# Mixers without zero-padded operands, heads in plane order, and small products issued in unbroken batches

## The chip, the cores and the metric

The kernel runs on one core of a Trainium2 chip. The metric is the device time of one execution in microseconds (us). Executions were repeated, and the median counts. Engines are named as in the profile: PE is TensorE, DVE VectorE, ACT ScalarE, POOL GpSimd, SP the engine that issues DMAs.

## What is computed

One layer of a streaming encoder, for 1024 new tokens of one stream and 32 tokens of a second, running stream: x plus a normed token mixer, then plus a normed causal ConvFFN. The mixer has three groups of heads side by side on one in-projection, and one out-projection behind them. Cut to what the change touches:

```python
# GLA (6 heads, 32 keys, 64 values) and HGRN2 (5 heads, 64 x 64): per chunk of 64 tokens
b = cumsum(log_a)                               # decay per key channel
scores = einsum('bihd,bjhd,bijhd->bijh', q, k, exp(b_i - b_j))   # for j <= i
o = scores @ v + (q * exp(b)) @ S
S = exp(b_last) * S + (k * exp(b_last - b)).T @ v
# mLSTM (5 heads, 64 x 64): per chunk, with a running maximum m
s = (q @ k.T) * w
num, den = s @ v + w0 * (q @ C), sum(s) + w0 * (q @ n)
h = num / max(|den|, exp(-m))
C, n = dc * C + (wk * k).T @ v, dc * n + sum(wk * k)
# every head: RMS norm, times a gate; then cat @ w_out
```

## The kernel before

**Stages.** The in-projection runs in three groups of tokens (0 to 383, 384 to 767, 768 to 1023 with the 32 sample tokens). Its large products are split into three fp32r products each (`mm3`, L100 to L102). In each group come first the blocks of features (`pf`: queries, keys, decays, written to DRAM as `qkb_d` and `mqk_d`), then the blocks by token (`pv`: values and gates, written to `v_d` and `g_d`). Then follow the out-projection (`zp`), the up-projection of the FFN as a Strassen product (`pu...`) and the down-projection (`pd`).

**Mixers.** A mixer is a generator that handles a unit of 128 tokens (two chunks of 64), unit 8 the 32 sample tokens. The order of units is 0, 1, 2, then 3, 4, 5, then 8, 6, 7. `merge` runs the mixers of one group's units beside the in-projection of the next group, and the last group's beside the out-projection: with each step of the main generator `pump` advances the mixers by a share of `NMIX` steps per unit (L1392). On this the scheduler of the program sets the final order per engine. A small product is recorded through `first` (L690 to L692, hence most are at L692), which raises its priority by AHEAD, 100.

**A unit.** It loads `qkb` (q, k and b of GLA and HGRN2, 768 KB, L703; one buffer), `mqk`, `v` and others. From b come `kh` (L758 to L761), transposed into `kt2`, and `qz` (L753). The scores within a chunk are formed by levels c = 32, 16, 8, 4, 2, 1: at each level b is taken relative to the middle of each block of 2c tokens (L802), then exponentials on ACT, then the two operands `Ld` (L807) and `Qz` (L813, L817) on DVE, 16 products into the bank pair `sc`, and a copy under a mask into `P` (`put`, L782). Only the second half of each block is a query, so a level's output has 32 columns per chunk and head. The diagonal, each token with itself, is a product `z` (L838), summed over keys into `sd` and copied into `P` too. Then come the updates of the state (`up` in the bank `mi`, S at L857 and L858), `P` times `v` into `og` (GLA) and `oh` (HGRN2), `qz` times the state into the same, and `finish` (ACT square, L888 sum, POOL power at L218 and L219, L890 product, L892 gate). Then the mLSTM: `sm` (scores), `w`, `kw2`, `um` (update of the memory), `om`, `oi`, `hn`, `finish`. The banks tagged "o" (`og`, `oh`, `sm`, `om`, `oi`) are two in all, `mi` is one bank of two halves.

**Padding.** A product whose head has 32 or 64 keys and uses part of the 128 rows has its operand padded with zeros to 128 rows: `qz` (11 heads), `mqz` (5), `kt2` and `kw2` (each chunk's tokens, zeros for the other chunk). So these products run on 128 rows by 64 or 32 columns; the levels run on 64 by 64.

## Time and profile before

| | |
|---|---|
| median of 3 runs | 1438.58 us (1437.68 to 1443.81) |
| span of the profiled execution, first to last instruction | 1434.5 us |
| mean granted TensorE clock in it | 0.984 |
| PE, DVE, ACT, POOL busy | 1370.8, 1008.9, 713.2, 274.1 us |
| mixers' small products in the trace | 187 to 635 us for the last level, first to last unit |

Of the profiled execution the profile gives the span alone; the three runs are other executions. How to read the lines below: a line of the timeline gives the start in us, the length, engine, line, operation, output and inputs, and the count of records put together. A line of a group gives, behind the count, busy time in all and the mean of one in ns, then the engine's idle time ahead of it and what ended it. In a product's line "64*64" is the part of the array that it uses, rows by columns, and an fp32 product shows as two records. Records of one engine overlap at their ends, so that the difference of two starts tells what one costs.

### The profile page before, as it was taken

The numbers are of one execution on the slowest core, as the hardware profiler recorded it, in microseconds if no ns is written. First come the engines' busy times: TensorE is split into PE (matmuls) and PEld (weight loads), VectorE is DVE, ScalarE is ACT, GpSimd is POOL, SyncE is SP. The second block draws the span as 40 slices with busy tenths as digits, with TensorE's granted clock in tenths as the row PEclk, the third lists the DMA queues.
The fourth block names the chain that finished last, engine by engine and source line by source line (L and its number), as shares of the span: only waits on it lengthen the run. The fifth ranks groups of instructions, "written<-read, shape, count | busy, mean of one in ns | idle before, by whom it ended". The sixth has DMA issues, their size and how long they took to land.

```text
span 1434.5 us, 30019 instructions
## 1 busy us (share of the span) xinstructions
PE 1370.8 (96%) x11804; PEld 1254.9 (87%) x11804; DVE 1008.9 (70%) x1826; ACT 713.2 (50%) x1403; POOL 274.1 (19%) x456
## 2 busy tenths in 40 slices
PE   7989999999998998999799999999999999999997
PEld 6989889898887986767699999999999999988785
DVE  5796478757596668676698888788878865654644
ACT  5545556445475545333665555455555545543432
POOL 6531121113021235212111111111111110000101
PEclk9999999999999999999899999999999999999999
DMA  9599778667789754344312221222122266665742
GB/s 344 190 317 351 263 251 300 221 228 241 236 279 329 250 181 148 109 147 111 122 49 98 79 90 61 90 75 82 68 90 75 75 211 227 222 214 170 247 168 103
DMA packets 132437, 255.11 MB, mean 178 GB/s; under 512 B 28647, under 2 KB 79367, under 8 KB 132295
## 3 DMA queue, kind: packets, MB, share of 16 engines
q1 hardware_dynamic: 132295, 253.19, 51.9%
q8 instruction: 92, 1.51, 0.4%
q14 instruction: 50, 0.41, 0.1%
HBM read 192.26 MB, written 60.89 MB: 176 GB/s over the span
## 4 chain that ended last, share of the span: by engine, by line
PE 73%; DVE 12%; ACT 5%; DMA 5%; issue 2%; POOL 1%; SPq 1%; DVEq 0%; ACTq 0%
PE pd L101 5%; PE pd L100 5%; PE pd L102 5%; PE pux L100 4%; PE pux L102 4%; PE pux L101 4%; PE pv L102 4%; PE pv L100 4%; PE pv L101 4%; PE puw L100 3%; PE puw L101 3%; PE puw L102 3%; DMA qkb<-qkb_d 2%; PE zp L100 2%; PE zp L101 2%
## 5 line engine op out<-in xcount | busy, mean ns | idle before, releaser
L1226 DVE SCALAR_TENSOR_TENSOR y<-uu,fconv_sb,y 128x1060 f32<-128x1060 f32 x88 | 116.2, 1321 | 27.4 <-ACT y L1224 26.6
L100 PE MATMUL pd<-wd,hh 128*128 128x512 f32 x264 | 104.5, 396 | 0.3 <-ACT hh L106 0.3
L101 PE MATMUL pd<-wd,hh 128*128 128x512 f32 x264 | 104.7, 397 | 0.0
L102 PE MATMUL pd<-wd,hl 128*128 128x512 f32 x264 | 90.5, 394 | 0.0
L1220 POOL COPY uu<-uu 128x2 f32<-128x2 f32 x44 | 30.5, 693 | 211.5 <-DVE uu L1188 211.4
L1183 ACT COPY c<-pux 128x274 f32<-128x274 f32 (+1 forms) x132 | 49.1, 375 | 41.4 <-PE pux L102 40.3
L1224 ACT ACTIVATE y<-uu,fconv_sb 128x1060 f32<-128x1060 f32 x44 | 56.1, 1275 | 18.6 <-POOL uu L1221 18.1
L100 PE MATMUL zp<-woh,ch 128*128 128x512 f32 (+1 forms) x144 | 58.3, 411 | 4.1 <-DVE cl L1020 3.1
L100 PEld LDWEIGHTS pd<-wd,hh 128*128 128x128 f32 x264 | 49.6, 188 | 13.1 <-ACT hh L106 0.9
L102 PEld LDWEIGHTS pd<-wd,hl 128*128 128x128 f32 x264 | 49.6, 188 | 11.9
L101 PEld LDWEIGHTS pd<-wd,hh 128*128 128x128 f32 x264 | 49.6, 188 | 11.5
L100 PE MATMUL pv<-wt_0h,xh 128*128 128x256 f32 (+2 forms) x195 | 57.1, 293 | 2.3 <-ACT xh L316 2.3
L101 PE MATMUL zp<-wol,ch 128*128 128x512 f32 (+1 forms) x144 | 58.6, 407 | 0.0
L102 PE MATMUL zp<-woh,cl 128*128 128x512 f32 (+1 forms) x144 | 58.0, 406 | 0.2 <-DVE cl L1020 0.2
L102 PE MATMUL pv<-wt_1h,xl 128*128 128x256 f32 (+2 forms) x195 | 56.9, 292 | 0.5 <-DVE xl L317 0.5
L102 PE MATMUL pv<-wt_0h,xl 128*128 128x256 f32 (+2 forms) x195 | 56.5, 290 | 0.6 <-DVE xl L317 0.6
L100 PE MATMUL pv<-wt_1h,xh 128*128 128x256 f32 (+2 forms) x195 | 56.7, 291 | 0.0
L101 PE MATMUL pv<-wt_1l,xh 128*128 128x256 f32 (+2 forms) x195 | 56.5, 290 | 0.0
L101 PE MATMUL pv<-wt_0l,xh 128*128 128x256 f32 (+2 forms) x195 | 56.2, 288 | 0.1
L101 PE MATMUL pd<-hl,wd 128*128 128x288 f32 x176 | 50.3, 297 | 0.6 <-DVE hl L109 0.6
L218 POOL TENSOR_SCALAR hrs<-hss 128x5 f32<-128x5 f32 (+3 forms) x27 | 13.9, 514 | 192.1 <-DVE hss L888 191.4
L102 PE MATMUL pd<-hh,wd 128*128 128x288 f32 x176 | 50.1, 296 | 0.0
(1668 smaller groups left out, 5162.7 us busy)
## 6 DMA issues: line engine op xcount, KB each, us to landing
h_d<-y SPq DMA_DIRECT2D x22, 530.0 KB, 2.9
wt_0r<-in_w_tok SPq DMA_DIRECT2D x21, 512.0 KB, 8.2
wt_1r<-in_w_tok SPq DMA_DIRECT2D x21, 512.0 KB, 5.6
wt_0l<-lt_d SPq DMA_DIRECT2D x14, 512.0 KB, 5.2
wt_1l<-lt_d SPq DMA_DIRECT2D x14, 512.0 KB, 4.6
qkb<-qkb_d SPq DMA_DIRECT2D x8, 768.0 KB, 6.3
hr<-h_d SPq DMA_DIRECT2D x44, 128.0 KB, 3.7
hr<-h_d SPq DMA_DIRECT2D x22, 192.0 KB, 3.3
```

The costliest lines, as they stand in the source:

```text
L100: pe.matmul(ps, lh[0], rh[0], start=first, stop=False, **kw)
L101: pe.matmul(ps, lh[0], rh[1], start=False, stop=False, **kw)
L102: return pe.matmul(ps, lh[1], rh[0], start=False, stop=last, **kw)
L218: pool.tensor_scalar(out, ss, 1.0 / width, EPS, op0=ALU.mult, op1=ALU.add)
L1183: act.copy(t, ps)
L1220: pool.tensor_copy(u[:, GAP_P:GAP_P + 2], u[:, GAP_S - 2:GAP_S])
L1224: act.activation(y, u, AF.Identity, scale=fconv[:, j, 2:3], bias=fconv[:, j, 3:4])
L1226: dve.scalar_tensor_tensor(y, uu[i][:, s:s + NCOL], fconv[:, j, s:s + 1], y, op0=ALU.mult, op1=ALU.add)
```

## The change

1. **Padding.** `qz`, `kt2`, `mqz`, `kw2` are gone. `qb` (L755, L757), `kt` and `kw` hold the operands once, and each product takes a slice of 64 rows (`up`: 64 rows by 32 columns, so that 22 products per unit become 32). Products of the two halves of the rows go to different banks (`up` one bank of `sc` per chunk, `sm`, `um`, `oi` two banks each, `og` for planes 0 to 5 and `oh` for 6 to 10). `P` times `v` and `om` keep their form.
2. **Plane order.** The 11 heads stand in the order of the planes of `P`; the columns of the weights are permuted on the host.
3. **Pairs.** `Ld` and `Qz` have four buffers. Two levels write side by side into one `sc` (32 columns each); their copies into `P` come behind both.
4. **Batches.** `batch` issues a pair's products and a group of others without a break: updates with `sm`; levels 32 and 16 with `um`; 8 and 4 with `oi` and `om`; 2 and 1 with `qb` times the state; and `P` times `v` alone, last. The diagonal comes behind the pair 2 and 1, `hn` ahead of it.
5. **Order.** AHEAD is 3000 instead of 100, NMIX 14 instead of 17. `mqk` comes in two loads instead of four.

```diff
-    Ld = [mx.tile([128, 4, 128], F32, name=f"Ld{i}") for i in range(2)]
-    Qz = [mx.tile([128, 6, 64], F32, name=f"Qz{i}") for i in range(2)]
-    qz = mx.tile([128, 11, 128], F32, name="qz")
-    kt2 = mx.tile([128, 2, 512], F32, name="kt2")
-    mqz = mx.tile([128, 5, 128], F32, name="mqz")
-    kw2 = mx.tile([128, 2, 5, 64], F32, name="kw2")
+    Ld = [mx.tile([128, 4, 128], F32, name=f"Ld{i}") for i in range(4)]
+    Qz = [mx.tile([128, 6, 64], F32, name=f"Qz{i}") for i in range(4)]
+    qb = mx.tile([128, 6, 128], F32, name="qb")
+    kt = mx.tile([128, 512], F32, name="kt")
+    kw = mx.tile([128, 5, 64], F32, name="kw")
...
-    AHEAD = 100
+    AHEAD = 3000
...
+        def batch(first_one, *rest):
+
+            gate = last = None
+            with tc.high_priority(offset=AHEAD):
+                gate = last = first_one()
+                with tc.issue_after(gate.ins):
+                    for part in rest:
+                        for one in part:
+                            last = one()
+            return last
...
-            spread(dve, qz, lambda r, fs, psl: dve.tensor_tensor(qz[r, psl, :n], q4[r, fs, :], eb4[r, fs, :],
-                                                                 op=ALU.mult), n)
+            dve.tensor_tensor(qb[:, 2:4, :n], eb4[:, 1:3, :], q4[:, 1:3, :], op=ALU.mult)
+            for i, f in enumerate((0, 3)):
+                dve.tensor_tensor(qb[:, 4 * i:4 * i + 2, :n], eb4[:, f:f + 1, :].broadcast_to([128, 2, n]),
+                                  qe[:, i, :, :n], op=ALU.mult)
...
+        ups = [mm(up[ch][r:r + 32, f, :], kt[o:o + m, 128 * f + r:128 * f + r + 32], v[o:o + m, 64 * p:64 * p + 64])
+               for p, (f, r0, dk) in reversed(list(enumerate(PLANES)))
+               for r in range(r0, r0 + dk, 32) for ch, (o, m) in enumerate(chunks)]
...
+        last = batch(ups[0], ups[1:], inner)
...
+        pairs = [levels[i:i + 2] for i in range(0, len(levels), 2)]
...
+        batch(lists[1][0], lists[1][1:], lists[0], inner)
+        for lv, c in enumerate(pairs[0]):
+            copy_scores(c, sc, lv)
...
+        last = batch(inter[0], inter[1:], *lists[::-1])
+        for lv, c in enumerate(pairs[2]):
+            copy_scores(c, sc, lv)
+        z = mx.tile([128, 512], F32, tag="x", name=f"x{u}_0", bufs=NX)
+        dve.tensor_tensor(z[:, :4 * n], q4.rearrange("p f n -> p (f n)"), k4.rearrange("p f n -> p (f n)"), op=ALU.mult)
+        sd = small(11)
+        with tc.issue_after(last.ins):
+            for f in range(4):
+                first(pe.matmul, sd[:n], z[:, f * n:f * n + n], of_head[:, f, :], start=f == 0, stop=f == 3)
+        put(0, sd[:n].unsqueeze(2).broadcast_to([n, 11, cl]))
...
+        intra = [mm(ots[p][0][o:o + m, ots[p][1], :], P[o:o + m, p, :m], v[o:o + m, 64 * p:64 * p + 64],
+                    start=False, stop=p in (5, 10)) for p in range(11) for (o, m) in chunks]
+        batch(intra[0], intra[1:])
...
-    NMIX, NIN = 17, 12 + 2 + 24
+    NMIX, NIN = 14, 12 + 2 + 24
```

How this moves instructions is seen at two places. On DVE between units 1 and 2, before: the copies of levels 2 and 1 (`sc1_2`, `sc1_1`) and of the diagonal (`mi`, 128x704) into `P`, the state S, and then `kh` of unit 2, which waits for the load of `qkb2`.

```order
L782 COPY_PREDICATED P_160<-masks_sb_108,sc1_2_3076 128x176x2 [waits PE_49]
L782 COPY_PREDICATED P_160<-masks_sb_108,mi_157 128x704 [waits DVE_49]
L389 SCALAR_TENSOR_TENSOR mo_1_2919<-th_1_2917,y_1_2912 128x384 [waits DMAHW0_49,Activation_49]
L782 COPY_PREDICATED P_160<-masks_sb_108,sc1_1_3135 128x352 [waits DVE_49,PE_49]
L858 TENSOR_TENSOR S1_0_3206<-S1_0_3206,mi_157 128x256 [waits PE_49]
L857 TENSOR_TENSOR S1_1_3220<-S1_0_3206,dec1_2780 128x256 [waits DVE_49]
L758 TENSOR_TENSOR kh2_3612<-qkb2_3556 128x512 [waits DMAHW6_49]
L802 TENSOR_TENSOR x2_32_3629<-qkb2_3556 128x512
```

The same place after the change (`sc1_2` is now the third bank pair, with levels 2 and 1; the copies are at L816, `kh` at L762 and L765, `qb` at L755 and L757):

```order
L937 TENSOR_TENSOR cat1_3334<-hn1_3337,hrs1_3336 128x320 [waits DVE_49,Pool_49]
L816 COPY_PREDICATED P_163<-masks_sb_108,sc1_2_3341 128x176x2 [waits PE_49]
L816 COPY_PREDICATED P_163<-masks_sb_108,sc1_2_3341 128x352 [waits DVE_49]
L762 TENSOR_TENSOR kh2_3699<-qkb2_3631 128x512 [waits DMAHW6_49]
L816 COPY_PREDICATED P_163<-masks_sb_108,mi_160 128x704 [waits DVE_49,PE_49]
L830 TENSOR_TENSOR x2_32_3830<-qkb2_3631 128x512
L749 COPY dec2_3694<-eb2_3692 128x8 [waits Activation_49]
L755 TENSOR_TENSOR qb_156<-eb2_3692,qkb2_3631 128x256
L757 TENSOR_TENSOR qb_156<-eb2_3692,qe2_3687 128x256 x2
L765 TENSOR_TENSOR kh2_3699<-kh2_3699,qkb2_3631 128x512 [waits Activation_49]
```

The subtraction for `kh2` now stands ahead of the copy of unit 1's diagonal. The same holds between units 2 and 3 and between 3 and 4; between 4 and 5, 8 and 6, and 6 and 7 the diagonal's copy stands ahead.

On PE, unit 2's last level and first update of the state before (`mi` from `v2` and `kt2`), inside big products (`pv`):

```order
L692 MATMUL sc2_1_3980<-Qz1_151,qkb2_3556 64x2x32 [waits DVE_49]
L692 MATMUL sc2_1_3980<-Qz1_151,qkb2_3556 64x2x32 x3
L692 MATMUL sc2_1_3980<-Qz1_151,qkb2_3556 64x32 x8
L692 MATMUL sc2_1_3980<-Qz1_151,qkb2_3556 64x2x32
L692 MATMUL sc2_1_3980<-Qz1_151,qkb2_3556 64x32
L692 MATMUL sc2_1_3980<-Qz1_151,qkb2_3556 64x2x32
L692 MATMUL sc2_1_3980<-Qz1_151,qkb2_3556 64x32
L692 MATMUL mi_157<-v2_3563,kt2_153 32x64 [waits DVE_49]
L692 MATMUL mi_157<-v2_3563,kt2_153 32x64 x5
L692 MATMUL mi_157<-v2_3563,kt2_153 64x64 x5
L102 MATMUL pv5_5_3839<-wt1_5_0h_3715,xl1_1716 128x256
```

After, the updates of both chunks come as one run of 32, with `sm` of both halves of the rows (`sm20`, `sm21`) behind them, ahead of all levels:

```order
L85 MATMUL pv4_3_3350<-wt1_3_1l_3303,xh1_1716 128x256
L780 MATMUL up2_3742<-v2_3636,kt_157 32x64 [waits DMAHW2_49,Activation_49]
L780 MATMUL up2_3742<-v2_3636,kt_157 32x64 x31
L780 MATMUL sm20_3740<-mqk2_3633 64x64 [waits DMAHW1_49,DVE_49]
L780 MATMUL sm20_3740<-mqk2_3633 64x64
L780 MATMUL sm21_3741<-mqk2_3633 64x64 [waits DVE_49,PE_49]
```

`sm20` waits for VectorE too: it takes a bank "o" that the unit before it frees with its `finish`. Over the whole program the places at which the big products are left for products of another tile fall from 120 to 73, and the changes of tile shape from 384 to 175. The mixers move closer together: counted in big products, unit 1 begins at 1329, 2 at 1460, 3 at 1607 and ends at 1689 (before 1200 to 1434, 1488 to 1752, 1776 to 2024), unit 0 lies between 596 and 692 (before 888 to 1131), and units 5, 8, 6 and 7 between 2396 and 2688 (before 2256 to 2823).

More of the change, by code (lines that the diff above doesn't have):

```diff
@@ L74 @@
 SCW = 88
-HCOL = [64 * (0, 2, 1, 3, 4)[i] for i in range(5)]
 VG0 = [range(0, 3), range(3, 6), range(6, 8)]
@@ L777, in put @@
+        yield
         def put(c, src):
[L778 removed]
+            mk_ = masks[:n, lev_index[c]:lev_index[c] + 1, :cl]
             dst = P[:n, :, :cl]
             if c:
[L781 to L788 removed]
@@ L790, in mixer, with level @@
-        li = 0
-        for c in levels:
+                mk_, dst, src = second(mk_, c), second(dst, c), src.rearrange("p h (b c) -> p h b c", c=c)
+            dve.copy_predicated(dst, mk_.broadcast_to([n, 11, *mk_.shape[2:]]), src)
+        def level(li, c, sc, lv):
             x = mx.tile([128, 512], F32, tag="x", name=f"x{u}_{c}", bufs=NX)
@@ L874, in mixer, with scores @@
-        if u in (7, 8):
-            sp.dma_start(a["p_gh" if u == 7 else "q_gh"], state["S", u == 8])
+                put(c, s[:n])
+        def scores(k):
+            sc = psm.tile([128, 1024], F32, tag="sc", name=f"sc{u}_{k}", bufs=1)
+            return sc[:, :11 * SCW].rearrange("p (h s) -> p h s", s=SCW)
+        pairs = [levels[i:i + 2] for i in range(0, len(levels), 2)]
+        ums = [psm.tile([128, 3, 65], F32, tag="o", name=f"um{u}{e}", bufs=2) for e in range(2)]
+        sc = scores(0)
@@ new lines, in mixer @@
+        lists = []
+        for lv, c in enumerate(pairs[0]):
+            lists.append(level(lv, c, sc, lv))
+            if not lv:
+                yield
+        inner = [mm(ums[ch][64 * (h % 2):64 * (h % 2) + 64, h // 2, :], kw[o:o + m, h, :], vmt[o:o + m, h, :])
+                 for h in range(5) for ch, (o, m) in enumerate(chunks)]
+        batch(lists[1][0], lists[1][1:], lists[0], inner)
+        for lv, c in enumerate(pairs[0]):
+            copy_scores(c, sc, lv)
+        yield
+        w = mx.tile([128, 320], F32, tag="w", name=f"w{u}", bufs=1)
@@ new lines, in mixer @@
+        if u in (7, 8):
+            sp.dma_start(a["p_c" if u == 7 else "q_c"], state["C", u == 8])
+        yield
+        sc = scores(1)
+        lists = []
+        for lv, c in enumerate(pairs[1]):
+            lists.append(level(2 + lv, c, sc, lv))
+            if not lv:
+                yield
+        ois = [psm.tile([128, 3, 65], F32, tag="o", name=f"oi{u}{e}", bufs=2) for e in range(2)]
+        om = small(5, 65)
+        inner = [mm(ois[h % 2][o:o + m, h // 2, :], mq[64 * (h % 2):64 * (h % 2) + 64, h // 2, o:o + m],
+                    Cs[ch][64 * (h % 2):64 * (h % 2) + 64, h // 2, :]) for h in range(5) for ch, (o, m) in enumerate(chunks)]
@@ L877, in mixer @@
+        inner += [mm(om[o:o + m, h, :], w[o:o + m, h * cl:h * cl + m], vmt[o:o + m, h, :])
+                  for h in range(5) for (o, m) in chunks]
+        batch(lists[1][0], lists[1][1:], lists[0], inner)
+        for lv, c in enumerate(pairs[1]):
+            copy_scores(c, sc, lv)
         yield
```

251 lines of the change are left out of this document (105 added, 146 removed).

## The prediction

> **What bounds the kernel now.** I read the page first: the span and the busy times.
>
> ```profile
> span 1434.5 us, 30019 instructions
> PE 1370.8 (96%) x11804; PEld 1254.9 (87%) x11804; DVE 1008.9 (70%) x1826; ACT 713.2 (50%) x1403; POOL 274.1 (19%) x456
> ```
>
> TensorE is the bound nearly everywhere, and VectorE has 30% of the span free on average. The change touches only the mixers, so I asked next for the busy times of two stretches in which mixers run: part of the second group's in-projection and the start of the third's (300 to 446 us), and the out-projection (517 to 679 us).
>
> ```profile
> core 0: us, PE busy (x) PEld busy (x) DVE busy (x) ACT busy (x) POOL busy (x), PEclk, DMA share, GB/s
> 300.00:446.00 146.00, 141.91 (x1880) 129.22 (x1879) 102.45 (x263) 76.99 (x169) 29.36 (x43) 0.99 0.77 255
> 517.00:679.00 162.00, 152.78 (x1494) 116.45 (x1493) 117.67 (x247) 68.39 (x152) 46.80 (x68) 0.96 0.44 144
> ```
>
> TensorE stands idle there for 4.1 and 9.2 us, 13.3 together; VectorE is busy for 70% and 73%, more than ScalarE or GpSimd. So what saves TensorE work here saves time, as long as VectorE, the next in line, keeps up. Third, the timeline of TensorE shows what the mixers' small products cost. This is the end of unit 2: its last level of scores, then updates of the state (mi<-v,kt), P·v, and the state's part of the output.
>
> ```profile
> 375.03 0.29 PE L101 MATMUL pf<-xl,wf_7h 128*128 128x288 f32 x1
> 375.26 0.69 PE L692 MATMUL sc<-Qz,qkb 64*64 64x64 f32 x32
> 375.87 0.92 PE L692 MATMUL mi<-v,kt 128*32 128x64 f32 x22
> 376.73 0.40 PE L102 MATMUL pf<-xh,wf_7l 128*128 128x288 f32 x1
> 376.96 0.30 PE L100 MATMUL pf<-xh,wf_7h 128*128 128x288 f32 x1
> 377.10 0.30 PE L101 MATMUL pf<-xl,wf_7h 128*128 128x288 f32 x1
> ...
> 379.33 0.33 PE L692 MATMUL og<-v,P 64*64 64x64 f32 x4
> ...
> 379.70 0.92 PE L692 MATMUL mi<-v,kt 128*32 128x64 f32 x22
> 380.55 0.27 PE L692 MATMUL og<-v,P 64*64 64x64 f32 x1
> ...
> 381.87 0.34 PE L692 MATMUL oh<-S,qz 128*64 128x64 f32 x4
> ...
> 383.34 0.40 PE L102 MATMUL pf<-xh,wf_7l 128*128 128x288 f32 x1
> ```
>
> Starts tell more than lengths, since the records overlap. A level of scores, tiles of 64 rows by 64 columns, takes 0.61 us for 32 records (each product has two), 19 ns each. The padded groups take 0.85 us for 22 records (39 ns), 1.32 for 38 (35 ns) and 1.47 for 44 (33 ns). Leaving and entering the big products costs too: from one big product to the next is 0.14 us, but 0.23 from the last big one to the first small one, and 0.23 again between the first two big ones behind. So one excursion into small products costs some 0.19 us beside the products.
>
> **The change on TensorE.** The mLSTM part of the same unit:
>
> ```profile
> 397.45 0.92 PE L692 MATMUL sm<-mqz,mqk 128*64 128x128 f32 x12
> 398.30 0.40 PE L102 MATMUL pf<-xh,wf_4l 128*128 128x288 f32 x1
> ...
> 399.60 0.33 PE L692 MATMUL oi<-C,mqz 128*64 128x65 f32 x2 [0.51 <-DVE cat L890]
> 399.97 0.56 PE L692 MATMUL mi<-vm,kw 128*64 128x65 f32 x10
> 400.46 0.40 PE L100 MATMUL pf<-xh,wf_4h 128*128 128x288 f32 x1
> ...
> 402.12 0.80 PE L692 MATMUL om<-vm,w 64*64 64x65 f32 x20
> 403.35 0.51 PE L692 MATMUL mi<-vm,kw 128*64 128x65 f32 x9 [0.43 <-DVE C L936]
> ...
> 404.31 0.41 PE L102 MATMUL pf<-xh,wf_5l 128*128 128x288 f32 x1
> ```
>
> One unit's small products now: six levels at 0.61 = 3.66; two state updates 0.86 + 0.85 = 1.71; P·v 0.37 + 1.32 = 1.69; the state's part 1.47; sm 0.85; oi and the mLSTM update 0.37 + 0.49 + 0.96 = 1.82; om 0.80. Together 12.0 us.
>
> After, every padded operand becomes a slice of 64 or 32 rows, so that the groups run in tiles like those of a level. Its 0.61 us less some 0.14 for entering and leaving are 15 ns per record. P·v and om keep their form, diagonal 64x64 tiles, and their rate; of their 1.32 us for 38 records I take 31 ns each. Then: updates and sm 64 + 20 records, 1.26 and 0.25 for entry and the change of tile = 1.5; levels 32 and 16 with the mLSTM update 84 records, 1.4; levels 8 and 4 with oi 84 and with om 20 at 31, 2.0; levels 2 and 1 with the state's part 108, 1.8; P·v 44 at 31, 1.5. Together 8.2 us, so 3.8 less; times 8.25 units (the sample unit is a quarter) 31 us. The order of instructions leaves big products for small ones 73 times instead of 120: 47 at 0.19 are 9 us. In all **-40 us** of TensorE work.
>
> The Trainium skill, "TensorEngine Tiling (Array Packing)", Key Properties, has it that changing the tiling mode, not just the tile, drains the engine. The order has 175 changes of tile shape instead of 384; if each of the 209 that go cost the 0.1 us seen at an entry, that would be 21 us in place of 9, and the sum 12 us lower. The trace agrees that entering and leaving cost 0.09 each; it doesn't show changes between two small shapes as dearer, since 0.61 for the level above holds the change to 128*32 behind it. I keep 9.
>
> **The change on VectorE.** The mixers' work there hardly shrinks. Of 28 groups from the first row below down to den, the busy times sum to 267 us; with the smaller ones 269, 32.6 per unit.
>
> ```profile
> L817 DVE TENSOR_TENSOR Qz<-x,qe 128x128 f32<-128x128 f32 (+1 forms) x106 | 29.8, 295 | 14.4 <-PE sc L692 14.2
> L753 DVE TENSOR_TENSOR qz<-qkb,eb 32x256 f32<-32x256 f32 (+7 forms) x54 | 20.2, 374 | 1.1
> L953 DVE SCALAR_TENSOR_TENSOR den<-hn 128x5 f32<-128x5 f32 (+1 forms) x9 | 1.4, 160 | 0.1
> 419.99 0.55 DVE L782 COPY_PREDICATED P<-masks_sb,sc 128x352 f32<-128x352 int32 x1
> 420.43 0.41 DVE L807 TENSOR_TENSOR Ld<-x,qkb 128x256 f32<-128x256 f32 x1
> 420.76 0.30 DVE L817 TENSOR_TENSOR Qz<-x,qe 128x128 f32<-128x128 f32 x1
> ```
>
> The second row, 6 instructions per unit and 2.4 us, becomes three writes without padding, some 1.2 us; four kw become two, 0.4 less. So 31 us by records. The last three rows show that records overlap by 0.08 to 0.11 us, so 55 instructions in a row take about 4.5 us less: **26.5 us per unit**. The six levels are still computed one by one; only their products come in pairs.
>
> What moves is where this work is due. With the lead of 3000 the mixers stand in the order close behind one another: units 1, 2 and 3 begin 131 and 147 big products apart, and the feature products of the next group have none beside them. A big product costs 0.12 us here:
>
> ```profile
> 306.25 0.28 PE L102 MATMUL pv<-wt_1h,xl 128*128 128x256 f32 x1
> 306.37 0.28 PE L100 MATMUL pv<-wt_1h,xh 128*128 128x256 f32 x1
> ```
>
> So TensorE has 139 x 0.119 = 16.5, 8.2 of small products and 1.6 of transposes and diagonals, **26.3 us per unit**. VectorE has 26.5 and some 2 for the projection's own blocks. That alone is 2 us short. Two waits come on top:
>
> ```profile
> L758 DVE TENSOR_TENSOR kh<-qkb 128x512 f32<-128x512 f32 (+1 forms) x9 | 6.4, 706 | 20.1 <-DMA qkb<-qkb_d 17.9 <-DMA qkb<-qkbs_d 2.2
> qkb<-qkb_d SPq DMA_DIRECT2D x8, 768.0 KB, 6.3
> L782 DVE COPY_PREDICATED P<-masks_sb,mi 128x704 f32<-128x704 int32 (+1 forms) x9 | 8.2, 911 | 0.2
> L219 POOL TENSOR_TENSOR hrs<-hrs,mhalf 128x5 f32<-128x5 f32 (+3 forms) x27 | 35.6, 1320 | 2.1
> ```
>
> The load of the next unit's qkb (one buffer) can start only behind the last pair of levels, and lands 6.3 us later. Three times VectorE's order holds the subtraction for kh, which waits for it, ahead of the copy of the diagonal into P, and P·v needs that copy: 6.3 + 0.7 + 0.9 = 7.9 us from pair to P·v. TensorE has 23 to 25 big products and the diagonal to fill it, 3.4 us: 4.5 us of stall. Before, the same wait (17.9 us in all) held only the next unit's first steps. Then sm of the next unit needs the banks of og and oh, which come free behind square, sum, the 1.3 us power on GpSimd and a product: some 3 us more than the products ahead of it cover, of which a part lies under the load, so I take 1.5. For units 1 to 3 this makes 2 + 4.5 + 1.5 = 8 us, **24 in all**.
>
> In the out-projection units 5, 8, 6, 7 stand between 2396 and 2688 in the count of big products: about 45 at 0.119 and 247 at the 0.23 us of these rows, plus 3.25 units at 9.8, is 94 us.
>
> ```profile
> 639.78 0.39 PE L100 MATMUL zp<-woh,ch 128*128 128x512 f32 x1
> 640.00 0.39 PE L101 MATMUL zp<-wol,ch 128*128 128x512 f32 x1
> L1056 DVE SCALAR_TENSOR_TENSOR z<-z,oss,gm 128x1024 f32<-128x1024 f32 (+1 forms) x8 | 11.0, 1377 | 1.6 <-POOL oss L219 1.6
> L1020 DVE TENSOR_TENSOR cl<-ctp,ch 128x512 fp32r<-128x512 f32 (+1 forms) x18 | 11.4, 636 | 5.1 <-ACT ch L1019 5.1
> ```
>
> VectorE has 3.25 x 26.5 = 86 there and, by the last two rows and lesser ones, some 5 us for each of five blocks: 111 or more, 17 over TensorE's; with the loads' waits, here behind the diagonal's copy, **18** (between 10 and 40).
>
> **The sum.** The profiled span 1434.5, less 40 of products, less the 13 of idle time that the two stretches have now (the new waits take their place), plus 24 + 18 = 42: 1423.5. The median of the runs, 1438.58, lies 4.1 over the span, which I add: 1427.6, taken as **1427**, 0.8% faster. Edits I cost at nothing: the weights' order is changed on the host; two loads of mqk instead of four and fewer memsets leave queues that nobody waits for; four ScalarE copies fewer per unit, since ScalarE is half idle; the second pair of Ld and Qz buffers only loosens waits. If the earlier hn chain did get in the way of level 2, it would cost its five rows, about 2 us a unit.
>
> **Rivals.** First, faster still: VectorE enters each burst ahead, because the feature phases leave it free and there are now four operand buffers, so only the three stalls behind the load (13.5) and some 5 us of the rest are left: 1434.5 - 53 + 18.5 + 4.1 = 1404. For it speaks that VectorE is short by 2 us a unit only; against it that no level can be made before its qkb has landed, and that buffer is single.
>
> Second, slower: VectorE becomes the bound of the bursts. A pair waits for both levels' operands, so the first level's copies into P, and with them the next pair, come later than when levels took turns; every unit then loses a further exp and its products, 3 to 4 us beside the 42, in all eight units: 1427 + 26 = 1453. It decides once VectorE's chain from pair to pair, not its sum, exceeds the 5 to 27 big products (0.6 to 3.5 us) that the order leaves between batches. Against it: the order has the operands' first steps ahead of the copies. The Trainium skill, "TensorEngine Tiling (Array Packing)", PSUM Bottleneck, warns of this: tiling speeds up TensorE but not the emptying of PSUM, which may become the bottleneck. The trace of before agrees only as far as VectorE's 73% in the out-projection.
>
> Third, that small products in 64-row tiles don't reach the level's rate: at the 33 ns of the padded groups nothing but the 9 us of entries would go, and waits would shrink with a TensorE less pressed; 1434.5 - 9 + 4.1 + about 10 = 1440. Against it stand the level's own 19 ns.
>
> **Chances.** My forecast 0.50 (own range 1413 to 1440), first rival 0.20, second 0.24, third 0.06. A measurement of this kernel can tell about 0.5%, 7.2 us, from no change. Faster than 1431.4: the first rival and 0.37 of the forecast, 0.57. Within: 0.13 of the forecast, the third rival and 0.02 of the second, 0.21. Slower: 0.22. The range that leaves out 2 in 10 goes from 1405, the middle of the first rival, to 1451, short of the second's middle.
>
> **What would show it.** Right: TensorE's busy time some 40 us lower; the padded groups gone, the state's part at 15 to 19 ns per record; between P·v of units 1, 2, 3 and what is ahead a wait of 3 to 5 us, put down to VectorE's P; VectorE busy 90% within the bursts and below before's in the feature phases. Wrong: TensorE waits under 25 us in all from 150 to 690 us (first rival); waits ahead of the first score product of each pair, put down to Qz or P, of over 2 us each (second); TensorE's busy time falling by under 15 us (third).

## The result, and the profile after

The changed kernel takes 1458.65 us (median of 4 runs, 1453.17 to 1460.62) beside 1439.55 of the kernel before in the same runs (4 runs, 1437.68 to 1443.81): a ratio of 1.011, 95% interval 1.0074 to 1.0146. It is **slower by 1.1%**, where 1427 was forecast. The profiled execution is the fastest of its four, 1453.17, with a span of 1451.4; before, the span was 1434.5.

The page of the changed kernel (span, busy time by engine, granted clock in 40 slices, and the chain that ended last by engine):

```profile
span 1451.4 us, 30420 instructions
PE 1343.1 (93%) x12042; PEld 1243.3 (86%) x12042; DVE 994.1 (68%) x1802; ACT 698.1 (48%) x1369; POOL 274.0 (19%) x453
PEclk9999999999999988899999999999999999999999
PE 71%; DMA 10%; DVE 9%; ACT 5%; issue 2%; POOL 2%; SPq 1%; DVEq 0%; ACTq 0%; POOLq 0%
```

TensorE is busy 27.7 us less than the 1370.8 before, yet the span is 16.9 longer, since it idles 108.3 us instead of 63.8. The third row has a dip, 8s from slice 15 to 17 (508 to 617 us), that a busy time does not tell of: there the clock of TensorE was lower, and the same products took longer.

To part these, I take each stretch of 2 us from the view by windows: its TensorE busy time, times one less the granted clock, is what the lower clock cost. What is left of the busy time is the work as it would be at full clock:

| us, one profiled execution | span | idle | lost to the clock | work at full clock |
|---|---|---|---|---|
| before | 1434.5 | 63.8 | 17.2 | 1353.5 |
| changed | 1451.4 | 108.3 | 34.4 | 1308.7 |
| difference | +16.9 | +44.5 | +17.2 | -44.8 |

So the products did get cheaper, by 45 us. All of it came back, and 17 more: 44.5 as idle time, 17.2 as clock. Where, the view by windows tells (span, then busy time of PE, PEld, DVE, ACT and POOL, the granted clock, the DMA share and GB/s); of the kernel before:

```profile
100.00:720.00 620.00, 589.39 (x6407) 517.59 (x6406) 428.30 (x969) 317.62 (x687) 137.18 (x201) 0.97 0.66 222
500.00:600.00 100.00, 93.22 (x920) 75.35 (x917) 74.49 (x170) 45.15 (x107) 33.31 (x41) 0.95 0.47 157
600.00:700.00 100.00, 93.61 (x851) 71.69 (x849) 71.13 (x131) 43.50 (x94) 24.54 (x45) 0.98 0.40 123
720.00:1300.00 580.00, 574.36 (x4404) 561.25 (x4403) 443.01 (x655) 293.38 (x523) 76.13 (x185) 1.00 0.33 114
```

and of the changed kernel:

```profile
100.00:720.00 620.00, 549.39 (x6575) 493.71 (x6573) 404.14 (x935) 290.85 (x627) 137.86 (x198) 0.94 0.66 220
500.00:600.00 100.00, 81.48 (x1065) 67.58 (x1064) 74.50 (x189) 39.93 (x99) 34.82 (x40) 0.87 0.44 138
600.00:700.00 100.00, 85.32 (x762) 64.52 (x761) 58.34 (x109) 34.59 (x79) 22.46 (x40) 0.89 0.40 123
720.00:1300.00 580.00, 570.17 (x4402) 560.07 (x4403) 443.65 (x652) 299.09 (x538) 77.59 (x189) 0.99 0.33 112
```

Most of the loss lies where the mixers run: from 100 to 720 us TensorE idles 70.6 us (620 less 549.4) instead of 30.6, at a clock of 0.94 instead of 0.97. That is 40.0 of the 44.5 us of idle time and, by the stretches of 2 us, 13.0 of the 17.2 of clock. The rest is small and stands behind 720. No engine is full there: VectorE, the suspect of the second rival, works 74.5 and 58.3 us in the two stretches of 100.

What TensorE waited for in the changed kernel (engine, output and line, what released it: us in all, times, longest):

```profile
PE og L780 <- DVE P L816: 21.5, 7, 4.8
PE xt L296 <- DVE x L285: 7.9, 1, 7.9
PE mi L670 <- DVE kh L765: 6.5, 4, 3.0
PE pv L86 <- DMA wt_1l<-lt_d: 5.3, 1, 5.3
PE ctp L1046 <- ACT z L1077: 5.0, 3, 4.5
```

The first row is new, and is half of the growth: P·v waits for the last copy into `P`. In the kernel before, no wait for `P` stands among the largest; its list began with the same 7.8 for `x` and then 4.0 for `vf`. What stands ahead of P·v on VectorE is seen in the timeline of unit 1, changed kernel:

```profile
275.78 0.49 DVE L935 TENSOR_REDUCE hss<-sq 128x5 f32<-128x320 f32 x1 [0.54 <-ACT sq L934]
277.86 0.49 DVE L937 TENSOR_TENSOR cat<-hn,hrs 128x320 f32<-128x320 f32 x1 [1.59 <-POOL hrs L203]
278.27 1.91 DVE L816 COPY_PREDICATED P<-masks_sb,sc 128x352 f32<-128x352 int32 x2
280.29 0.69 DVE L762 TENSOR_TENSOR kh<-qkb 128x512 f32<-128x512 f32 x1
280.90 0.93 DVE L816 COPY_PREDICATED P<-masks_sb,mi 128x704 f32<-128x704 int32 x1
```

The last pair's products ended at 275.1. VectorE then finishes `hn` and stands still 1.59 us for GpSimd's power, makes two copies, starts the next unit's `kh` and only then copies the diagonal, until 281.83. Before, the same place of unit 1 looked like this:

```profile
263.14 0.69 PE L692 MATMUL sc<-Qz,qkb 64*64 64x64 f32 x32
263.75 0.92 PE L692 MATMUL mi<-v,kt 128*32 128x64 f32 x22
264.61 0.38 PE L102 MATMUL pv<-wt_1h,xl 128*128 128x256 f32 x1
...
266.93 0.33 PE L692 MATMUL og<-v,P 64*64 64x64 f32 x4
```

There one copy (263.90, 0.94 us) stands between, and the updates and 18 big products lie over it. Summed over the nine units, from the last score product to the first P·v product: before 34.9 us, all but 0.5 filled by other products of TensorE; changed 59.3 us, of which 37.9 filled.

The clock often falls at such waits. Changed kernel, unit 5, windows around the longest wait:

```profile
506.00:508.00 2.00, 0.00 (x0) 0.00 (x0) 1.47 (x4) 1.35 (x6) 0.65 (x1) 1.00 0.00 0
508.00:509.00 1.00, 0.00 (x0) 0.00 (x0) 1.00 (x3) 0.00 (x0) 0.00 (x0) 1.00 0.00 0
509.00:510.00 1.00, 0.00 (x0) 0.00 (x0) 1.00 (x3) 0.00 (x0) 0.00 (x0) 0.69 0.00 0
510.00:512.00 2.00, 1.97 (x36) 1.97 (x38) 1.53 (x9) 1.48 (x7) 0.19 (x1) 0.50 0.00 0
...
514.00:516.00 2.00, 2.00 (x10) 2.00 (x10) 1.57 (x8) 0.83 (x4) 1.99 (x2) 0.50 0.19 57
516.00:517.00 1.00, 1.00 (x9) 1.00 (x8) 0.80 (x6) 0.00 (x0) 0.84 (x3) 0.89 0.00 0
```

TensorE stands from 505.2 to 510.0, and from 509.4 (0.69 of that window is half 0.50, half 1.00 by time) to 516.2 every product runs at 0.50. That is 6.8 us at half clock behind a wait of 4.8: the wait is paid again by up to 3.1 us (0.5 times the 6.2 us in which TensorE then works). In the whole execution the clock is at half in 15 stretches in which TensorE has work, before in 8. A wait is not the whole cause: the 2.51 us ahead of unit 0's P·v (to 145.7) brought no drop, and in the kernel before the clock fell at 522.8 with TensorE busy for 3.0 of the 3.4 us ahead, in unit 8's small products, and no wait over 0.3 us.

### The profile page after: what moved, and what is told of

Read it like the earlier page. It is cut to its first block, busy times and chain, and to the rows that moved or that the text cites. A ratio compares the mean times of both kernels' runs of the same rounds, so it can differ in the third digit from the quotient of the medians.

```text
span 1451.4 us, 30420 instructions
## 1 busy us (share of the span) xinstructions
PE 1343.1 (93%) x12042; PEld 1243.3 (86%) x12042; DVE 994.1 (68%) x1802; ACT 698.1 (48%) x1369; POOL 274.0 (19%) x453
## 4 chain that ended last, share of the span: by engine, by line
PE 71%; DMA 10%; DVE 9%; ACT 5%; issue 2%; POOL 2%; SPq 1%; DVEq 0%; ACTq 0%; POOLq 0%
PE pd L84 5%; PE pd L85 5%; PE pd L86 5%; PE pux L84 4%; PE pux L86 4%; PE pux L85 4%; PE puw L84 3%; PE puw L85 3%; PE puw L86 3%; DMA qkb<-qkb_d 3%; PE pv L84 3%; PE pv L86 3%; PE pv L85 2%; PE zp L86 2%; PE zp L84 2%
## 5 line engine op out<-in xcount | busy, mean ns | idle before, releaser
L1256 DVE SCALAR_TENSOR_TENSOR y<-uu,fconv_sb,y 128x1060 f32<-128x1060 f32 x88 | 116.3, 1322 | 27.7 <-ACT y L1254 26.9
L84 PE MATMUL zp<-woh,ch 128*128 128x512 f32 (+1 forms) x144 | 61.6, 429 | 2.8 <-DVE cl L1050 1.8
L405 POOL TENSOR_TENSOR vg<-vth,gh 128x256 f32<-128x256 f32 (+1 forms) x36 | 34.3, 952 | 126.5 <-DVE vth L402 88.5
```

The lines of the kernel that those rows point to most:

```text
L84: pe.matmul(ps, lh[0], rh[0], start=first, stop=False, **kw)
L405: pool.tensor_tensor(o[:n], th[:n], gh[:n, c0:c0 + 256], op=ALU.mult)
L1256: dve.scalar_tensor_tensor(y, uu[i][:, s:s + NCOL], fconv[:, j, s:s + 1], y, op0=ALU.mult, op1=ALU.add)
```

## Theories

My theory after the profile was **the tail**: load, finish and copies between the last pair and P·v cost the 21.5 us of waits and the clock behind them. Its rivals: **the close order** (AHEAD 3000, NMIX 14); **VectorE as a whole**, the second rival of the prediction (theory 1 in the expectations for thin); and **an outrun chain**: TensorE waits for a chain of the other engines that has a length of its own, so that products saved return as idle time (theory 3 in the later expectations; theory 4 there is its opposite).

## Experiments: the order and the tail

**lead_low**: the changed kernel with the lead of before and its 17 steps per unit, batches still unbroken.

```diff
+    LEAD = 100        # first of a batch, and single products
-    NMIX, NIN = 14, 12 + 2 + 24
+    NMIX, NIN = 17, 12 + 2 + 24
```

> The changed kernel with the lead of 100 and NMIX 17 of before for the first product of each batch and for single products; the rest of a batch keeps the lead of 3000, so batches stay unbroken (67 excursions). Units spread out again (unit 1 at 1329 to 1416, 2 at 1476 to 1608, 3 at 1790 to 1938). Theory A, the close order makes VectorE and the loads late: idle time of TensorE back from 108 to 65 to 80 us, its busy time at 1330 to 1345, the time 1400 to 1425. Rival B, the pairs and batches themselves (a pair waits for two levels' operands): idle time stays over 95 us, time 1440 to 1460. Rival C, the granted clock falls for another reason than the waits: clock stays at 0.97, idle falls, time 1425 to 1445.

Measured 1458.01 beside 1444.37 before, ratio 1.0101 [1.0065, 1.0137]; waits before P·v 26.2 us. No gain: the close order is not what holds the changed kernel back.

**before_close**: the kernel before with AHEAD = 3000 and NMIX = 14, all else as it was.

```diff
-    AHEAD = 100
+    AHEAD = 3000
-    NMIX, NIN = 17, 12 + 2 + 24
+    NMIX, NIN = 14, 12 + 2 + 24
```

> The kernel before with the changed kernel's lead of 3000 and NMIX of 14 alone: padding, single levels and small batches as before. Theory A, the close order is what costs: TensorE's idle time rises from 64 by 20 us or more, time 1455 to 1480. Rival B, pairs and batches are what costs: within 10 us of before, 1432 to 1450.

Measured 1457.89, ratio 1.0096 [1.0066, 1.0126], idle time 78.4. In the old kernel this order costs as much as the whole change; in the new one its removal returns nothing. The two losses don't add.

**b_apart**: `b` loaded ahead into a tile with two buffers, so that `kh` doesn't wait (`Ld` gives up one of its four buffers).

```diff
-        qkb = mx.tile([128, 1536], F32, tag="qkb", name=f"qkb{u}", bufs=1)
+        bt = mx.tile([128, 512], F32, tag="bt", name=f"bt{u}", bufs=2)
+        qkb = mx.tile([128, 1024], F32, tag="qkb", name=f"qkb{u}", bufs=1)
```

> The changed kernel with b of qkb in a tile of its own with two buffers, loaded a unit ahead (and three Ld buffers instead of four, for the room); q and k are loaded as before. The subtraction for kh, the exponentials and the levels' first steps no longer wait for the load. Theory A: waits of P times v for P and of the kh transposes for kh, 21.5 and 8.7 us, fall under 10 together, time 1430 to 1445. Rival B: the levels still wait in pairs, time 1450 to 1460.

Measured 1461.43, ratio 1.0125 [1.0107, 1.0143]; waits before P·v 25.3. This is no proof against the load, as VectorE's timeline of unit 1 in it shows:

```profile
276.69 0.96 DVE L820 COPY_PREDICATED P<-masks_sb,sc 128x352 f32<-128x352 int32 x1
279.12 0.43 DVE L759 TENSOR_TENSOR qb<-eb,qkb 128x256 f32<-128x256 f32 x1 [1.47 <-DMA qkb<-qkb_d]
279.46 0.68 DVE L769 TENSOR_TENSOR kh<-kh,qkb 128x512 f32<-128x512 f32 x1
280.06 0.93 DVE L820 COPY_PREDICATED P<-masks_sb,sc 128x352 f32<-128x352 int32 x1
```

`q` and `k` still come into one buffer, and with `b` early, the next unit's `qb` moved in between the copies and waited there for the load (2.60 us in unit 3). Two buffers for all of `qkb` weren't tried; for those of `b` alone, `Ld` gave up one of its four.

**diag_early**: the diagonal behind the pair 8 and 4. Its sum overwrites a part of `om` that `hn` had not read, so the mLSTM's output is another.

```diff
+        # behind the pair 8, 4:
+        dve.tensor_tensor(z[:, :4 * n], q4..., k4..., op=ALU.mult)
+        ...
+        put(0, sd[:n].unsqueeze(2).broadcast_to([n, 11, cl]))
```

> The changed kernel with the diagonal's product, sum and copy one step earlier, behind the pair 8 and 4 instead of behind 2 and 1; everything else as in the changed kernel. The load of the next unit is then no longer ahead of a copy that P times v needs. Theory A: the wait of P times v for P, 21.5 us in all, falls under 6, idle time by 10 to 16, time 1437 to 1448. Rival B: the wait moves to the next pair's products, idle time within 5 of 108, time 1452 to 1460.

Measured 1467.15, ratio 1.0168 [1.014, 1.0196]. Waits before P·v fell to 9.6, and those of the transposes for `kh` rose from 6.5 to 16.5.

**fin_late**: `hn`'s maximum, reciprocal, sum of squares, power and product held behind the diagonal's copy.

```diff
+        with tc.issue_after(diag.ins):
+            dve.scalar_tensor_tensor(den[:n, :5].unsqueeze(2), hd, -1.0, hd, op0=ALU.mult, op1=ALU.max)
```

> The changed kernel with hn's denominator, norm and gate on VectorE behind the diagonal's copy into P instead of ahead of the three copies: the 1.6 us that VectorE stands waiting for GpSimd's power, and some 1.5 us of products, are no longer between the last pair and P times v. Theory A: P times v waits 8 to 14 us less in all (21.5 now), time 1440 to 1452. Rival B, VectorE's whole chain per unit bounds the bursts: the wait moves to the next unit's kh transposes or sm, time 1453 to 1462.

Measured 1453.5 beside 1441.39, ratio 1.0086 [1.0063, 1.011]. P·v waits 5.9 us instead of 21.5, in the third row below, which names `den`, the instruction behind the diagonal's copy (fin_late):

```profile
PE xt L296 <- DVE x L285: 8.2, 1, 8.2
PE pv L84 <- DVE vth L402: 6.6, 3, 2.9
PE og L780 <- DVE den L975: 5.9, 2, 3.1
```

The two waits left are the mechanism that the prediction named. In unit 1 VectorE now reaches the next unit's `kh` before its load has landed, and the diagonal's copy stands behind it (fin_late; P·v starts at 285.06):

```profile
283.46 0.69 DVE L762 TENSOR_TENSOR kh<-qkb 128x512 f32<-128x512 f32 x1 [3.34 <-DMA qkb<-qkb_d]
284.07 0.93 DVE L816 COPY_PREDICATED P<-masks_sb,mi 128x704 f32<-128x704 int32 x1
```

In unit 5 `kh` waits 2.12 us in the same way. Idle time in all fell from 108.3 to 102.5 only.

**tail_clean**: as fin_late, and the next unit's first steps that need its load (`dec`, `qb`, `kh`) also behind that copy.

```diff
+            if "diag" in state:
+                behind.enter_context(tc.issue_after(state["diag"].ins))
```

> The changed kernel with the finish of hn held behind the diagonal's copy, as in fin_late, and also the next unit's first steps on VectorE that wait for its load (the decay's copy, qb, the subtraction for kh) held behind that copy. Between the last pair's products and P.v VectorE then has three copies and nothing else. The waits before P.v (21.5 us in the changed kernel) should be under 5 us. If the tail is where the new order loses its time, as the run without it says (19 us), the kernel comes to 1438 to 1446; if the held steps are themselves needed at once by TensorE (the transposes of kh, hn's group), the waits move there and it comes to 1448 to 1456.

Measured 1456.07 beside 1442.41, ratio 1.0098 [1.0072, 1.0124]. (The profiled execution, at 1468.08, is 10 us over the other four of this kernel.) The place itself is mended: 41.0 us between last score and P·v in nine units, all filled. But (tail_clean):

```profile
PE mi L670 <- DVE kh L770: 13.4, 5, 4.7
PE pv L84 <- DVE vth L402: 8.7, 4, 3.0
PE xt L296 <- DVE x L285: 8.0, 1, 8.0
PE ctp L1052 <- ACT z L1083: 6.0, 3, 5.5
```

The held `kh` is now late itself, and idle time is 108.9 as in the changed kernel. In diag_early and tail_clean what was taken away at the tail came up at `kh`, and in fin_late 15.6 us less of waits before P·v left only 5.8 less idle time: the tail is where the largest waits are, but not what sets their sum.

**no_tail** left level 1's copy, the diagonal's product, sum and copy out.

```diff
         for lv, c in enumerate(pairs[2]):
-            copy_scores(c, sc, lv)
-        z = ...
-        put(0, sd[:n].unsqueeze(2).broadcast_to([n, 11, cl]))
+            if not lv:
+                copy_scores(c, sc, lv)
```

> The changed kernel without what stands behind the last pair's products: the copy of level 1, the diagonal's product on VectorE, its four products on TensorE and its copy into P are left out (some 4 us of VectorE in each unit); level 2's copy stays and releases P.v. The waits before P.v, 21.5 us in 7, should fall below 10. If these waits with the half-clock windows that follow them cost what they seem to (21.5 and some 10), the time falls by 15 to 30 us. If the wait only moves to the next thing, as it did with the diagonal ahead and with the finish behind, it falls by less than 8.

Measured 1438.19 beside 1442.38, ratio 0.9968 [0.995, 0.9986], 1.4% or some 20 us under the changed kernel by the two ratios. That looks like the upper case. But waits before P·v fell to 6.7 and idle time only from 108.3 to 104.5, clock loss from 34.4 to 33.8. Work at full clock fell by 11.4, from 1308.7 to 1297.3: the gain is first the left-out products, 72 records fewer that were busy for 8.9 us in the changed kernel, with their visits to the mixer; the rest lies in 4.4 us of idle time and clock and in the executions (the profiled one of the changed kernel was 5.5 under its median).

**fill**: five products of 256 columns into the bank of the scores ahead of P·v, in eight units, to keep TensorE busy.

```diff
+            for i in range(5):
+                first(pe.matmul, fill[:, :256], ident, v[:, :256], start=True, stop=True)
```

> The changed kernel with five more products per full unit (ident times a part of v, 128x256, about 0.4 us each) right ahead of P times v, into the banks of scores once level 1 is copied; they compute nothing that is used. They fill about 2 of the 1.4 to 4.8 us that TensorE waits there. Theory C, a wait of more than some 3 us lowers the granted clock to one half for about 7 us: with the waits split the clock lost falls by 5 to 12 us, time 1443 to 1455 although work is added. Rival: the clock loss hangs on something else, and the filler's 16 us count in full or nothing changes: 1456 to 1475.

Measured 1472.22, ratio 1.021 [1.0191, 1.0229]. Work rose by 16.0, idle time fell by 3.1, the clock's loss rose from 34.4 to 39.6. Filling didn't bring the clock back. It is a weak test: the fillers waited for VectorE themselves, 10.9 us in five units, so they stood behind the waits more than in them.

## Experiments: pairs, VectorE, and TensorE's own work

**single** and **single_low**: levels one at a time as before, each unbroken with another group; lead 3000 and NMIX 14, or 100 and 17. In both, unit 8's diagonal falls on `om`, so the sample tokens' output is another.

```diff
-        batch(lists[1][0], lists[1][1:], lists[0], inner)
-        for lv, c in enumerate(pairs[0]):
-            copy_scores(c, sc, lv)
+        single(0, pairs[0][0])
+        yield
+        single(1, pairs[0][1], inner)
```

> The changed kernel with its levels singly instead of in pairs: unpadded operands, plane order, unbroken batches, lead 3000 and NMIX 14 stay; the updates of the mLSTM go with level 16, oi and om with 4, the state's part with 1; each level's copy follows its product, the diagonal comes behind level 2 as before the change. From levels to P times v only one copy is left instead of three. Theory A, the changed kernel loses by long waits behind the pairs (idle 108 us, and with each wait over 3 us some 3.4 us at half the clock): idle falls to 75 to 95, clock from 0.968 to 0.975 or more, time 1425 to 1445. Rival B, the lead and the close order make the waits whatever the levels' grouping: time 1450 to 1465. Rival C, more excursions (94 instead of 73) eat the gain: busy time up by 10 or more.

> As the kernel with single levels, but with the lead of 100 for the first product of a batch and for single products, and NMIX 17, so that units spread as before the change. Theory A (pairs): as with single levels or better, 1415 to 1440. Rival B (close order): clearly faster than the kernel with single levels and close order, by 10 us or more. If neither the pairs nor the close order matter, 1450 to 1465 again.

Measured 1448.47 and 1449.93 beside 1441.39: ratios 1.0052 [1.0031, 1.0073] and 1.006 [1.0039, 1.0081]. **single2**, the same with unit 8's diagonal ahead of level 2:

```diff
-            if c == 2:
+            if c == 2 and u < 8:
                 diag()
```

> The changed kernel with levels of scores one at a time as before, each level's products issued unbroken with the other group, without padded operands and with the heads in plane order; the diagonal has its place behind level 2's copy, in a bank of its own time. If the pairs are what costs (three copies behind the last pair instead of two), 6 to 12 us less than the changed kernel, 1446 to 1451; if the time is set by total work of TensorE plus waits that any close order has, within 5 us of the changed kernel.

Measured 1447.8 beside 1443.69, ratio 1.0026 [1.0008, 1.0043]. The gap before P·v is 38.1 us in nine units, 37.1 of it filled. So the pairs, with the diagonal behind the last of them, cost about 0.8% of the 1.1%, and unpadded products with unbroken groups, for 40 us less work, bring nothing.

Two versions add the held steps to it. **single2_fin** holds `hn`'s finish behind the last copy, **single2_clean** the next unit's first steps too.

```diff
+        end = state["diag"] = copy_scores(pairs[2][-1], sc, 0)
+        with tc.issue_after(end.ins):
+            dve.scalar_tensor_tensor(den[:n, :5].unsqueeze(2), hd, -1.0, hd, op0=ALU.mult, op1=ALU.max)
```

> The kernel with levels one at a time, unbroken groups and no padding, and the finish of hn (maximum, reciprocal, sum of squares, power, product) held behind the last copy into P. The waits before P.v go, as in the changed kernel with the finish behind; the gain there was 2 to 4 us. Expected 1441 to 1448 beside 1443 before: a kernel no faster than before by more than 0.3% either way. Theory 3 gives nothing beyond that; theory 4 would give the whole of these waits, 8 to 12 us, and a kernel faster than before.

> Levels one at a time with unbroken groups and without padding, finish of hn and the next unit's load-dependent steps both held behind the last copy into P. There the gap before P.v was covered already (31.6 us, none idle), so the held steps can only move: 1443 to 1452, no faster than before. A result under 1438 would say that the next unit's steps had been in the way of more than P.v.

Measured 1447.8 beside 1442.38 and 1445.72 beside 1442.41: 1.0037 [1.0019, 1.0054] and 1.0029 [1.0013, 1.0044]. No version that leaves nothing out beats the kernel before.

**thin** and **before_thin**: the copies of levels 16, 8 and 4 into `P` left out, in the changed kernel and in the kernel before. The 23 us that the expectation takes from the 0.95 us of a copy are too many: these 26 copies were busy for 13.4 us in the changed kernel, and VectorE's busy time falls by 10.2 us there and by 9.3 in the kernel before.

```diff
-            else:
+            elif c < 4:
                 put(c, s[:n])
```

> The changed kernel without the copies of the scores into P for the levels 16, 8 and 4: three copies under a mask in each unit are left out (the first level's, the last pair's second copy and the diagonal's stay), so P holds the first level's sums there. VectorE loses 3 x 0.95 us in 8 units, about 23 us, some of it in the last stretch before P.v; TensorE keeps every product. Theory 1 (after the change VectorE's chain sets the pace of the mixers, the second rival of the prediction): the time falls by most of that, 20 to 35 us with the half-clock windows that go with the waits, to 1422 to 1438. Theory 2 (no one engine; with TensorE 50 us lighter, waits for all of them come up in a fixed order): 5 to 12 us, to 1446 to 1453, VectorE's busy time falls by 23 and TensorE's idle by at most half of that.

> The kernel before without the same three copies in each unit. Both theories: 0 to 6 us, to 1435 to 1441, since TensorE waited little there (63.7 us idle in the span). Were it as much as in the changed kernel's run, the copies would be no more a bound after the change than before it, and theory 1 would fall.

Measured 1464.48 and 1425.82 beside 1443.69: 1.016 [1.0126, 1.0194], and 0.9886 [0.9858, 0.9913]. Neither theory foresaw this. In the changed kernel VectorE's relief brings nothing at all, which speaks against VectorE as a whole (theory 1). It doesn't refute it alone, since VectorE's order changed too: in unit 4 `kh` of the next unit stands ahead of the `finish` in thin and behind it in the changed kernel, VectorE waits 9.1 us for the load instead of 6.1, and TensorE waits 10.6 us for `kh`. The waits before P·v are 23.9. In the kernel before the relief brings 18 us; its profiled execution accounts for 9.1 of them, as 2.0 of idle time, 4.5 of clock and 2.6 of work.

**before_less** and **after_less**: the state's part of `og` and `oh` left out.

```diff
-            first(pe.matmul, ot[o:o + m, OUT[h], :], qz[:, h, o:o + m], Ss[ch][:, f, :],
-                  start=False, stop=h == h1 - 1, skip_group_check=True)
```

> The kernel before without the products of the state's part of the mixers' output (og and oh from Qz and S: 44 small products in each of the units with two chunks of rows, about 12 us of TensorE in all); the other engines keep all their work and the order stays. If TensorE sets the time before the change: 10 to 13 us less, about 1427 to 1430. If even there work taken from TensorE comes back as waits and as half-clock windows: under 5 us less, and the idle time grows by over 5.

> The changed kernel without the products of the state's part of the mixers' output (og and oh from S and qb), as in the run on the kernel before that left out this part: about 16 us less of TensorE; the other engines keep their work. Theory 3: the time falls by less than 5 us, the idle time rises by 10 or more. Theory 4: the time falls by 13 to 18 us, as it did in the kernel before.

Measured 1424.8 beside 1443.69 (0.9881 [0.9853, 0.991]) and 1446.05 beside 1442.38 (1.0029 [1.0015, 1.0044]). Before: work fell by 17.8, the time by 19 (12.8 in the profiled execution, where the clock took 4.7). Changed: work fell by 6.4 only, of the 16 that the busy times of the two groups (8.4 and 7.8) had let me expect; idle time stayed at 108.4, and the time fell by 0.8% or some 12 us by the two ratios. In both, work left out is time gained, and none of it turned to idle time: the outrun chain (theory 3) falls from this side.

**after_more**: every score product issued twice.

```diff
-            for j in range(4):
+            for j in (0, 0, 1, 1, 2, 2, 3, 3):
```

> The changed kernel with every product of the scores issued twice (the second writes the same sums over the first), within the same unbroken groups: 28 to 30 us more of TensorE, nothing more for any other engine. Theory 3 (TensorE has outrun a chain of the other engines; the idle time is slack of it): most of it is absorbed, the time rises by 0 to 12 us from the changed kernel's 1457, and the idle time falls by 15 to 30 from 108. Theory 4 (the stalls belong to the new order and come on top of whatever TensorE does): the time rises by 25 to 32 us and the idle time stays within 8 us of 108.

Measured 1527.62 beside 1442.38, ratio 1.0577 [1.0535, 1.0619]: 4.7% or 67 us over the changed kernel for 20.6 us of work. Outside every theory; idle time rose from 108.3 to 149.6, the clock's loss from 34.4 to 47.4. VectorE's timeline of one unit in it:

```profile
510.37 0.69 DVE L762 TENSOR_TENSOR kh<-qkb 128x512 f32<-128x512 f32 x1 [15.61 <-DMA qkb<-qkb_d]
510.98 0.93 DVE L816 COPY_PREDICATED P<-masks_sb,sc 128x352 f32<-128x352 int32 x1
```

Here the next unit's subtraction stands ahead of the first copy, waits 15.6 us for its load, and TensorE waits 16.5 for `P`: in this order the mechanism that the prediction named, where it had 4.5 for a unit. The waits before P·v are 53.9 us in all. The run says that TensorE is not free beside a longer chain. As a price of work it doesn't count, since the order changed with it.

## What the runs leave of the theories

| us, one profiled execution | span | idle | lost to the clock | work at full clock |
|---|---|---|---|---|
| before, before_thin, before_less | 1434.5, 1425.4, 1421.7 | 63.8, 61.8, 64.0 | 17.2, 12.7, 21.9 | 1353.5, 1350.9, 1335.7 |
| before_close | 1458.7 | 78.4 | 31.6 | 1348.7 |
| changed | 1451.4 | 108.3 | 34.4 | 1308.7 |
| lead_low, b_apart, fin_late | 1457.4, 1459.3, 1449.6 | 116.8, 113.0, 102.5 | 36.6, 41.8, 38.1 | 1304.0, 1304.4, 1309.0 |
| single2, single2_fin, single2_clean | 1444.9, 1441.0, 1443.1 | 97.1, 97.1, 99.1 | 34.8, 30.1, 29.9 | 1313.0, 1313.7, 1314.1 |

Every kernel with the new products idles 97 to 117 us and loses 30 to 45 to the clock, whatever was moved or left out (diag_early and the profiled run of tail_clean 50; after_more, with products added, 149.6 and 47.4), and every one with the old order idles 62 to 64 and loses 13 to 22. Shown are: the work saved, the idle time and clock that ate it, the tail as the place of the largest waits, and that mending the tail mostly moves them. Not settled is what holds the idle time at about 100 us. Levels taken singly (97.1 in single2) and the old lead (98.9 with both, in single_low) leave it there, so the unbroken groups and the cheaper products themselves remain as the largest parts of the change; no run has the unpadded products without unbroken groups. One candidate for the chain behind it stands in the view of the chain that ended last. In the kernel before the load of `qkb` stands on it four times (start, us; the first and the last):

```profile
191.27 7.37 DMA qkb<-qkb_d
...
441.61 7.12 DMA qkb<-qkb_d
```

In the changed kernel, seven times (the first two and the last):

```profile
140.60 6.85 DMA qkb<-qkb_d
275.14 5.13 DMA qkb<-qkb_d
...
588.48 5.65 DMA qkb<-qkb_d
```

Five of the seven start within 1.3 us of the end of a unit's last pair (275.14 and 275.1 in unit 1), whose products and the diagonal are the last to read the single buffer. So units now follow each other through the load: last pair, load, levels, last pair. That chain runs through TensorE's own groups as well. It would fit that a wait mended at one point appears at the next, and that work left out of a group is gained. This is argued from the chain, not shown, and one number speaks against it: VectorE's `kh` waits for this load 14.0 us in the changed kernel, less than the 20.1 before, and 24.5 in fin_late with less idle time. The run that would show it needs a second full `qkb`.

## Why the prediction was wrong

Two steps of the sum failed: the idle time, put at 29 us more and measured at 44.5, and the clock, which had no term and cost 17.2.

- **Products, -40.** Right in mechanism and a little small: 44.8 at full clock. The updates run at 15 ns per record and the state's part at 17 to 24 (units 2, 4 and 1), not at the 33 of the third rival, which is out. The busy time alone (-27.7) would have misled, as 17.2 of the saving stands in it as slower clock.
- **Idle time that goes, -13, and waits that come, +42: together +29.** Measured +44.5. The step that failed: the prediction let the idle time of two stretches vanish with TensorE's saving, but from 100 to 720 us it went from 30.6 to 70.6.
- **P·v behind load and diagonal, 13.5 in units 1 to 3.** The place and the engine were right, its size was not: 2.9, 1.4 and 3.9 us, 8.2 in all, but four other units waited too (2.5, 1.6, 4.8, 4.4), 21.5 together. And the load was the smaller part of the cause: `kh` waited for it 0, 0.7 and 0.6 us there. The prediction counted one copy and the `kh` behind the load; two more copies and a finish that waits 1.6 us for GpSimd stood in the same 6.7 us.
- **VectorE short by 2 us per unit, and 17 in the out-projection.** Failed: VectorE is busy for 76% from 262 to 352 us (68.8 of 90), where units 1 to 3 run, and for 58 to 75% from 500 to 700. Sums of an engine's work over a stretch were the wrong measure; the waits that were looked at one by one came from what stood in front in VectorE's order.
- **The clock.** The sum had no term for it: 17.2 us, the largest error. The span forecast was 1423.5; 4.8 more saved, 15.5 more idle time and 17.2 of clock make the measured 1451.4. The Trainium skill, "TensorE: Matmul & The Clock Gate", HAM oscillation, tells of the case: an engine that waits between its groups falls to half clock and starts each next group cold. The trace agrees in the half clock (0.50 in the rows above) and differs in the wait that it takes: the page's rule has idle gaps over some 3.4 us, and here the clock fell 1.5 us into a wait of 2.42.

The rows for that (changed kernel, windows):

```profile
528.00:529.00 1.00, 0.40 (x4) 0.16 (x2) 1.00 (x4) 1.00 (x2) 0.67 (x2) 1.00 0.73 123
529.00:530.00 1.00, 0.00 (x0) 0.00 (x0) 1.00 (x2) 1.00 (x3) 0.36 (x1) 0.93 0.80 263
530.00:532.00 2.00, 1.11 (x4) 0.71 (x4) 2.00 (x4) 1.15 (x4) 0.00 (x0) 0.50 0.85 213
```

TensorE stops at 528.4 and goes on at 530.8; the clock falls at 529.9, with TensorE busy for 2.0 of the 3.4 us ahead.

- **The rivals.** The second came near in time (1453) by another mechanism than its own: the waits before a pair's first score product stayed small (2.1 us in all on VectorE's C), and VectorE as a bound fits neither its busy share nor thin, whose order changed as well. The Trainium skill, "TensorEngine Tiling (Array Packing)", PSUM Bottleneck, warns that emptying PSUM may become the limit. thin left out three of a unit's copies from PSUM and gained nothing, so no run here shows their amount as the limit.

## What to carry to other kernels

Before counting a cheaper product as time, split the span into idle time, clock and work, and ask what will lie over each wait once the cheaper engine gets there sooner: here 45 us of saved work were repaid in full by idle time and half clock. When work is put into unbroken groups, count everything that stands on the other engines between one group and the next, in their order and with their own waits, and not their total. A mended wait is a gain only if the idle time falls with it.

## What the hardware showed that I had not expected

- Half clock comes in stretches of 3.4 us or a multiple of it: in the changed kernel 6 of 3.4, 8 of 6.8 (509.4 to 516.2 behind a wait of 4.8, 529.9 to 536.7 in one of 2.42) and one of 10.2; in the kernel before 6 of 3.4, one of 6.8 and one of 13.7.
- Issuing products of 64 by 64 twice in the same groups (20.6 us of work) cost 67 us, and taking 13 us of copies off VectorE gained nothing in one kernel (ratio 1.016 beside 1.011) and 18 us in the other. In after_more and thin the order changed as well.
